# Fewer input buffers, more output buffers, stores held back: a WKV recurrence on one core

## The chip, the cores and the metric

The kernel runs on one core of a Trainium2 chip. Its time is the device time of one execution in microseconds; the median of three runs counts. All data start and end in HBM.

## What is computed

The reference is the WKV recurrence of an RWKV layer, for 16 batches, 2048 steps and 256 channels, all float32. Each batch and channel has a running numerator `aa`, a running denominator `bb` and a running maximum `pp` that keeps the exponentials in range:

```python
for t in range(seq_len):
    kk, vv = k[b, t], v[b, t]
    ww = u + kk
    qq = np.maximum(pp, ww)
    e1, e2 = np.exp(pp - qq), np.exp(ww - qq)
    output[b, t] = (e1 * aa + e2 * vv) / (e1 * bb + e2 + 1e-08)
    ww = pp - w + kk
    qq = np.maximum(ww, kk)
    e1, e2 = np.exp(ww - qq), np.exp(kk - qq)
    aa, bb, pp = e1 * aa + e2 * vv, e1 * bb + e2, qq
```

So an output is a quotient of two weighted sums over all earlier steps, with weights that are exponentials of k and of the decay w. k and v are 33.6 MB each, and so is the output: 100.7 MB have to pass between HBM and the core's memory.

## The kernel before

**Tiles.** The 2048 steps are cut into 16 chunks of 128 steps (the partitions), the 16 batches into four groups of four. Tile n is chunk n // 4 and group n % 4, so there are 64 tiles of 128 steps x 4 batches x 256 channels, 512 KB in float32. A tile of k, one of v and one of the output go through the core for each n.

**The work on a tile.** `load_k` and `load_v` bring it in (tiles `kr`, `vr`). VectorE copies k to the matmul's number format (`round_k`, L176, result `km`) and v to bfloat16 (`cast_v`, L209, result `vb`). TensorE adds the decay to k by matmuls (`logs`, L185 and L191), ScalarE takes the exponential (`exps`, L202 and L204) into the ring `EZR`, which keeps the last 12 tiles, and VectorE multiplies by v (`times_v`, L214). `sums` (L238) adds a chunk up for the state, and a chain of small steps, from `copy_sums` to `state_next`, carries the state to the next chunk and puts it into a spare row of the `EZR` tiles by four small DMAs (`inject`, L331). Ten slots after `exps` (LAG) the tile is finished: the denominator by matmuls with a triangular matrix (`den`, L341), its inverse on ScalarE as exp(-log) (`den_log` L346, `den_exp` L349, tile `rd`), the numerator by matmuls (`num`, L358), the product on VectorE (`mult`, L362, in place in `rd`) and `store` (L365).

**Loops and order.** A slot is one pass of one of two loops: n from 0 to 9, which only fills the ring, and n from 10 to 63, which also finishes tile q = n - 10 (and multiplies tile qp = n - 11). After slot 63 a tail written out by hand finishes tiles 53 to 63. Every instruction is issued in the order written (`K`), each engine works its own list from the front, and engines wait for each other by semaphores. Thus SyncE (SP), which issues all loads and all stores except two halves at the end, works one list too: at the head of slot n come `load(n + AHEAD)`, that is v(n + 5) and k(n + 6), and then `store(qp - 2)`, the store of tile n - 13. The last state injection goes through SyncE as well, the other ones through GpSimd.

**Buffers.** Tiles come from pools. A load into a buffer waits until the earlier tile in it has been read: `kpool` has AHEAD = 6 buffers, `vpool` 5. `rpool` has 8 `rd` buffers; the logarithm that opens a new `rd` waits until the earlier output in that buffer has been stored. Each of these tiles takes 4 KB of every partition, so the three pools hold 19 tiles together. k(n + 2) is copied in slot n, so a buffer of k is free two slots ahead of its number; v is cast unevenly: tiles with n % 4 of 3 and 0 in slot n, those with 1 and 2 in the slot before. Beside the buffers, each DMA of SyncE waits until the eighth one before it has landed, as eight semaphores are used in turn.

**The end.** Tile 63 is finished in two halves, so that its last bytes leave soon. For each half: exponential of that half of the denominator on ScalarE, multiply on VectorE, then two stores of 128 KB, one issued by SyncE and one by ScalarE (L533).

Of the kernel before, what the change touches and what calls it, by code (L numbers as in the profile page):

```python
# [15 lines left out]
def kernel(  # L16
# [16 lines left out]
    D = 2 * Dm  # L33
    NP = 4 * NST
    RING = 12
    AHEAD = 6
    LAG = 10
    RS = 2.0 ** -20
    CAP = 54.0
# [1 line left out]

    consts = ctx.enter_context(tc.tile_pool(name="consts", bufs=1))
    kpool = ctx.enter_context(tc.tile_pool(name="kpool", bufs=AHEAD))
    vpool = ctx.enter_context(tc.tile_pool(name="vpool", bufs=5))
    vbpool = ctx.enter_context(tc.tile_pool(name="vbpool", bufs=4))
    rpool = ctx.enter_context(tc.tile_pool(name="rpool", bufs=8))
    small = ctx.enter_context(tc.tile_pool(name="small", bufs=2))
    tiny = ctx.enter_context(tc.tile_pool(name="tiny", bufs=1))
    ps = ctx.enter_context(tc.tile_pool(name="ps", bufs=1, space=bass.MemoryType.PSUM))
# [4 lines left out]
    def rows_of(x, n):  # L54
        c, p = divmod(n, 4)
        return x[4 * p:4 * p + 4, c * TC:(c + 1) * TC, :].rearrange("n t d -> t n d")

    def load_k(n, queue=SP):
        kr_of[n] = kpool.tile([128, 4, Dm], F32, tag="kr", name="kr")
        K(queue.dma_start(out=kr_of[n], in_=rows_of(k, n)))  # L60

    def load_v(n, queue=SP):
        vr_of[n] = vpool.tile([128, 4, Dm], F32, tag="vr", name="vr")
        K(queue.dma_start(out=vr_of[n], in_=rows_of(v, n)))


    def load(n):
        if n - 1 < NP:
            load_v(n - 1)
        if n < NP:  # L70
            load_k(n)
# [37 lines left out]
    load_v(0)  # L109
    for n in range(2, AHEAD):  # L110
        load_k(n)
# [36 lines left out]
    def out_matrices(*names):  # L148
        if "L" in names:
            for h in range(2):  # L150
                fill(Lx[HS * h:HS * h + HS, HS * (1 - h):HS * (2 - h)], 0.0)
        for name in names:
            x, f = I1 if name[0] == "I" else Lx, RS if name[-1] == "N" else 1.0
            mats[name] = matrix(name, BF16)
            K(DVE.tensor_single_scalar(mats[name], x, f, op=ALU.mult))
# [18 lines left out]
    def round_k(n):  # L174
        km = consts.tile([128, 4, Dm], F32R, tag=f"km{n % 2}", name="km") if n < 2 else KM[n - 2]
        K(DVE.tensor_copy(km, kr_of.pop(n)))  # L176
        KM[n] = km

    def logs(n):
        km = KM[n].rearrange("p (i n) d -> p i (n d)", i=2)  # L180

        def rows(q):
            for i in range(2):
                g = 32 * (2 * q + i)
                K(PE.matmul(half(n, q)[:, i, :], CO[g:g + 32, :],  # L185
                            WU[g:g + 32, :].unsqueeze(1).broadcast_to([32, 2, Dm]), start=True, stop=False,
                            tile_position=(g, 0), skip_group_check=True))

        def steps(q):
            for i in range(2):  # L190
                K(PE.matmul(half(n, q)[:, i, :], (NLE, NLZ)[q], km[:, i, :], start=False, stop=True,  # L191
                            skip_group_check=True))

        rows(0)
        rows(1)
        steps(0)
        steps(1)

    def exps(n):
        if n < TURNS:  # L200
            for q in range(2):
                K(SC.activation(ez(n)[:, q], half(n, q), ACT.Exp))  # L202
        else:
            K(SC.activation(ez(n)[:, 0:2], PS[:, 0:4, :].rearrange("p (q i) x -> p q i x", q=2), ACT.Exp))  # L204

    def cast_v(n):
        vb = vbpool.tile([128, 4, Dm], BF16, tag="vb", name="vb")
        vr = vr_of.pop(n)
        K(DVE.tensor_copy(vb, vr))  # L209
        VB[n] = vb  # L210

    def times_v(n):
        vb = VB.pop(n).rearrange("p (i n) d -> p i (n d)", i=2)
        K(DVE.tensor_mul(ez(n)[:, 2:4], ez(n)[:, 0:2], vb.unsqueeze(1).broadcast_to([128, 2, 2, D])))  # L214
# [16 lines left out]
    def sums(n):  # L231
        c, p = divmod(n, 4)
        t = MISC[:, 0:Dm]
        for o in range(2):
            x = 24 - 16 * o - 2 * p
            for j in range(4):
                q, i = divmod(j, 2)
                K(PE.matmul(t[32 * j:32 * j + 32, :], mats["OH"][:, x:x + 32],  # L238
                            ez(n)[:, 2 * q, i, Dm * o:Dm * o + Dm],
                            start=p == 0 and o == 0, stop=p == 3 and o == 1,  # L240
                            tile_position=(0, 32 * j), skip_group_check=True))

    def copy_sums(c):
        ts = tiny.tile([128, Dm], F32, tag="ts", name="ts")
        if c == NST - 1:
            K(DVE.tensor_copy(ts, MISC[:, 0:Dm]))
        else:
            K(SC.activation(ts, MISC[:, 0:Dm], ACT.Copy))
        st[c, "ts"] = ts
# [88 lines left out]
    def den(n, bank=DENB):  # L338
        for m, q in (("L", 0), ("Id", 1)):
            for i in range(2):  # L340
                K(PE.matmul(bank[:, i, :], mats[m], ez(n)[:, q, i, :], start=q == 0, stop=q == 1,  # L341
                            skip_group_check=True))
# [5 lines left out]
    def den_exp(n, i=slice(0, 2)):  # L348
        K(SC.activation(RD[n][:, i, :], RD[n][:, i, :], ACT.Exp, scale=-1.0))  # L349

    def recip(n, between):
        den_log(n)
        between()
        den_exp(n)

    def num(n, bank, i):
        for m, q in (("LN", 2), ("IdN", 3)):
            K(PE.matmul(bank, mats[m], ez(n)[:, q, i, :], start=q == 2, stop=q == 3, skip_group_check=True))  # L358

    def mult(n, bank, i):  # L360
        rd = RD[n]
        K(DVE.tensor_mul(rd[:, i, :], bank, rd[:, i, :]))  # L362

    def store(n):
        K(SP.dma_start(out=rows_of(out, n), in_=RD.pop(n).rearrange("p i (n d) -> p (i n) d", n=2)))  # L365
# [22 lines left out]
    def small_work(n, where):  # L388
        for f, c in later.pop((n, where), []):
            f(c)  # L390
# [13 lines left out]
    for n in range(LAG):  # L404

        load(n + AHEAD)
        exps(n)
# [14 lines left out]
        if n < 4:  # L422
            (state_start, lambda: out_matrices("L"), lambda: out_matrices("IdN", "LN"),
             lambda: out_matrices("Id"))[n]()

    def inverses(n):
        q, qp = n - LAG, n - LAG - 1
        if qp >= 0:
            num(qp, NUMB, 1)

        sums(n - 1)
        if n + 1 < NP:
            recip(q, lambda: small_work(n, "recip"))

    for n in range(LAG, NP):

        q, qp = n - LAG, n - LAG - 1
        load(n + AHEAD)

        if qp >= 2:  # L440
            store(qp - 2)
        if qp >= 0:
            num(qp, NUMB, 0)
        den(q)
        small_work(n, "nums")
        exps(n)
        small_work(n, "act")
        if qp >= 0:
            mult(qp, NUMB, 0)
        small_work(n, "mid")  # L450
        if n == LAG:

            inverses(n)
            small_work(n, "early")
        if n + 2 < NP:
            round_k(n + 2)

        if n % 4 in (3, 0):
            cast_v(n)
        if n + 1 == NP:  # L460
            times_v(n)
        elif n % 4 < 2:
            cast_v(n + 1)
        if n > LAG:
            inverses(n)
        if qp >= 0:
            mult(qp, NUMB, 1)
        small_work(n, "scan")
        if n + 1 < NP:
            times_v(n)  # L470
            small_work(n, "chain")
            logs(n + 1)
        small_work(n, "pe")
# [4 lines left out]
    q, c = NP - LAG - 1, NST - 1  # L478
# [10 lines left out]
    den(q + 1, dbank(q + 1))  # L489
    sums(NP - 1)  # L490
    copy_sums(c)
    store(q - 2)
    store(q - 1)
    den_exp(q)
    den_log(q + 1, dbank(q + 1))
    tile_num(q, 0)
# [30 lines left out]
    n, p = NP - 1, (NP - 1) % 4  # L527
    for i in range(2):
        den_exp(n, slice(i, i + 1))
        mult(n, nbank(n, i), i)  # L530
        for j, eng in ((0, SP), (1, SC)):
            b = 4 * p + 2 * i + j
            K(eng.dma_start(out=out[b, c * TC:(c + 1) * TC, :], in_=RD[n][:, i, Dm * j:Dm * j + Dm]))  # L533
# [31 lines left out]
```

## Time and profile before

| | |
|---|---|
| time, median of 3 runs (lowest, highest) | 289.56 us (289.51, 289.62) |
| span of the profiled run | 288.0 us |
| busy: VectorE, TensorE, ScalarE | 262.3, 261.4, 254.7 us (91, 91, 88%) |
| HBM read, written | 67.12 MB, 33.55 MB |
| mean rate over the span | 350 GB/s |
| DMA issues of 512 KB | 64 of k, 64 of v, 63 of the output |
| median from issue to landing: k, v, output | 8.3, 8.3, 8.1 us |
| last k: issued, copied | 242.1, 250.4 us |
| last multiply starts | 283.5 us |

The time is that of an unprofiled run, the span goes from the first to the last instruction of the profiled one, so the two differ by some 1.5 us. Three engines and the DMA engines are all busy for most of the span; which of them holds up the others changes along the way, so the profile has to be read by stretches. A DMA has three times in the trace: the issue (an instruction on SyncE, ScalarE or GpSimd), the packets on the 16 DMA engines, and the landing, when its semaphore is complete. In a timeline the two numbers ahead of an instruction are its start and its busy time in us, SPq and ACTq are the DMA issues of SyncE and ScalarE, and a bracket behind it gives the idle time of the engine just before and the instruction that ended it.

### The profile page before, as it was taken

Reading aid. Unit: us, or ns where it says so; the run is one execution under the profiler, and the core shown is the slowest. Engines: PE = TensorE matmul, PEld = TensorE weight load, DVE = VectorE, ACT = ScalarE, POOL = GpSimd, SP = SyncE. Lnnn points to the kernel's source line nnn. Section 1 sums busy time; section 2 is a strip of 40 time slices with the busy share of each in tenths; the row PEclk is TensorE's granted clock in tenths of the full one; section 3 lists DMA queues with packets and bytes.
Section 4 is the critical chain, followed back from the end, with each engine's and each line's share of the span. In section 5 each row is a group of like instructions: output and inputs, shape, how many; then the busy total and the mean of one; then the engine's idle time right before and its main releaser. Section 6 shows DMA issues by size and latency. Waiting matters only on the chain. (4 is left out here: it accounts for less than half of the span.)

```text
span 288.0 us, 5023 instructions
## 1 busy us (share of the span) xinstructions
PE 261.4 (91%) x1694; PEld 119.4 (41%) x1694; DVE 262.3 (91%) x463; ACT 254.7 (88%) x252; POOL 105.2 (37%) x208
## 2 busy tenths in 40 slices
PE   5997897999999999999999999899998989998990
PEld 1443443544444544435444444344344444433430
DVE  4698999999999999999999999998999999988863
ACT  2675678999999999999999989999998999998891
POOL 7000523352534454543525364460434435233000
PEclk9799999999999999999999999999999999999997
DMA  6999999999999999999999999999999999994697
GB/s 214 353 348 350 349 331 349 331 361 375 381 369 381 372 379 378 381 379 381 378 376 381 369 381 375 377 376 371 373 374 380 374 377 380 373 383 160 201 339 245
DMA packets 103587, 101.54 MB, mean 353 GB/s; under 512 B 4285, under 2 KB 103561, under 8 KB 103561
## 3 DMA queue, kind: packets, MB, share of 16 engines
q1 hardware_dynamic: 101336, 100.45, 102.6%
q0 software_dynamic: 1920, 0.50, 0.8%
q8 instruction: 13, 0.21, 0.3%
q10 hardware_dynamic: 304, 0.27, 0.3%
q14 instruction: 14, 0.11, 0.1%
HBM read 67.12 MB, written 33.55 MB: 350 GB/s over the span
## 5 line engine op out<-in xcount | busy, mean ns | idle before, releaser
L204 ACT ACTIVATE EZR<-PS 128x2048 bf16<-128x2048 f32 x54 | 101.2, 1875 | 7.5 <-PE PS L191 6.5
L362 DVE TENSOR_TENSOR rd<-PS,rd 128x512 f32<-128x512 f32 x128 | 87.0, 687 | 6.1 <-ACT rd L349 4.7
L214 DVE TENSOR_TENSOR EZR<-EZR,vb 128x2048 bf16<-128x2048 bf16 x64 | 78.1, 1220 | 2.2 <-ACT EZR L202 1.5
L349 ACT ACTIVATE rd<-rd 128x1024 f32<-128x1024 f32 (+1 forms) x65 | 67.9, 1047 | 2.7 <-DVE rd L362 1.8
L346 ACT ACTIVATE rd<-PS 128x1024 f32<-128x1024 f32 x64 | 65.7, 1026 | 0.8 <-PE PS L341 0.8
L358 PE MATMUL PS<-EZR,LN 128*128 128x512 bf16 x128 | 48.7, 381 | 12.2 <-DVE rd L362 8.4
L331 POOL DMA_DIRECT2D EZR<-cb x60 | 36.5, 614 | 52.1 <-DVE cb L326 45.4
L176 DVE CAST km<-kr 128x1024 fp32r<-128x1024 f32 x64 | 44.7, 699 | 6.9 <-DMA kr<-in_k_dram 6.4
L191 PE MATMUL PS<-km,NLE 128*128 128x512 f32 x128 | 47.5, 453 | 2.3 <-DVE km L176 2.2
L358 PE MATMUL PS<-EZR,IdN 128*128 128x512 bf16 x128 | 48.4, 378 | 0.0
L209 DVE CAST vb<-vr 128x1024 bf16<-128x1024 f32 x64 | 43.4, 694 | 0.7 <-DMA vr<-in_v_dram 0.7
L191 PE MATMUL PS<-km,NLZ 128*128 128x512 f32 x128 | 40.6, 398 | 0.0
L341 PE MATMUL PS<-EZR,Id 128*128 128x512 bf16 x128 | 38.1, 379 | 0.0
L341 PE MATMUL PS<-EZR,L 128*128 128x512 bf16 x128 | 38.1, 379 | 0.0
L185 PE MATMUL PS<-WU,CO 32*128 32x512 bf16 x256 | 27.2, 388 | 3.4 <-DVE WU L400 2.2
L269 POOL TENSOR_TENSOR F<-LL,LL 128x32 f32<-128x32 f32 x13 | 6.7, 515 | 61.9 <-ACT LL L260 61.9
L191 PEld LDWEIGHTS PS<-km,NLZ 128*128 128x128 f32 x128 | 24.4, 191 | 5.8
L191 PEld LDWEIGHTS PS<-km,NLE 128*128 128x128 f32 x128 | 19.3, 190 | 17.3 <-issue 12.9
L238 PE MATMUL PS<-EZR,OH 128*32 128x256 bf16 x512 | 26.1, 278 | 0.1
L202 ACT ACTIVATE EZR<-PS 128x1024 bf16<-128x1024 f32 x20 | 19.4, 1019 | 7.6 <-PE PS L191 7.6
L358 PEld LDWEIGHTS <-IdN 128*128 128x128 bf16 x128 | 12.5, 97 | 28.7 <-issue 26.3
L282 POOL TENSOR_TENSOR Q<-P,F 128x64 f32<-128x64 f32 x13 | 15.7, 1205 | 15.0 <-DVE P L273 15.0
(71 smaller groups left out, 200.0 us busy)
## 6 DMA issues: line engine op xcount, KB each, us to landing
kr<-in_k_dram SPq DMA_DIRECT2D x64, 512.0 KB, 8.3
vr<-in_v_dram SPq DMA_DIRECT2D x64, 512.0 KB, 8.3
out_dram<-rd SPq DMA_DIRECT2D x63, 512.0 KB, 8.1
EZR<-cb POOLq DMA_DIRECT2D x60, 8.0 KB, 5.3
out_dram<-rd SPq DMA_DIRECT2D x2, 128.0 KB, 2.7
out_dram<-rd ACTq DMA_DIRECT2D x2, 128.0 KB, 2.2
EZR<-cb SPq DMA_DIRECT2D x4, 8.0 KB, 1.9
wuf<-in_w_dram ACTq DMA_DIRECT2D x1, 8.0 KB
```

The costliest lines, as they stand in the source:

```text
L176: K(DVE.tensor_copy(km, kr_of.pop(n)))
L185: K(PE.matmul(half(n, q)[:, i, :], CO[g:g + 32, :], WU[g:g + 32, :].unsqueeze(1).broadcast_to([32, 2, Dm]), start=True, stop=False, tile_p ...
L191: K(PE.matmul(half(n, q)[:, i, :], (NLE, NLZ)[q], km[:, i, :], start=False, stop=True, skip_group_check=True))
L204: K(SC.activation(ez(n)[:, 0:2], PS[:, 0:4, :].rearrange("p (q i) x -> p q i x", q=2), ACT.Exp))
L209: K(DVE.tensor_copy(vb, vr))
L214: K(DVE.tensor_mul(ez(n)[:, 2:4], ez(n)[:, 0:2], vb.unsqueeze(1).broadcast_to([128, 2, 2, D])))
L331: K(queue.dma_start(out=EZR[r:r + 1, 2 * q, r0:r0 + 4, :, :].rearrange("o p i (b x) -> o (p i b) x", b=4), in_=cb[x:x + 32, :]))
L341: K(PE.matmul(bank[:, i, :], mats[m], ez(n)[:, q, i, :], start=q == 0, stop=q == 1, skip_group_check=True))
L346: K(SC.activation(RD[n], bank, ACT.Ln, scale=RS))
L349: K(SC.activation(RD[n][:, i, :], RD[n][:, i, :], ACT.Exp, scale=-1.0))
L358: K(PE.matmul(bank, mats[m], ez(n)[:, q, i, :], start=q == 2, stop=q == 3, skip_group_check=True))
L362: K(DVE.tensor_mul(rd[:, i, :], bank, rd[:, i, :]))
```

## The change

The three pools keep their 19 tiles, divided otherwise: four for k, four for v, eleven for outputs. Loads go out four slots ahead (three for v). Stores are held back: at the head of slot n the tile n - 18 is stored instead of n - 13. Once no loads are left (from slot 61) three stores a slot are issued, of tiles whose product is ready, until they have caught up, and the tail stores what is left. The purpose is to give the loads the place in SyncE's queue that early stores took, and to leave stores for the end, when nothing is loaded. Besides, at the very end both exponentials of tile 63 are issued ahead of its first multiply and its stores.

```diff
-    AHEAD = 6
+    AHEAD = 4
+    OUTS = 11
+    LATE = 7
...
-    vpool = ctx.enter_context(tc.tile_pool(name="vpool", bufs=5))
+    vpool = ctx.enter_context(tc.tile_pool(name="vpool", bufs=AHEAD))
     vbpool = ctx.enter_context(tc.tile_pool(name="vbpool", bufs=4))
-    rpool = ctx.enter_context(tc.tile_pool(name="rpool", bufs=8))
+    rpool = ctx.enter_context(tc.tile_pool(name="rpool", bufs=OUTS))
...
+    stored = 0
+
...
         q, qp = n - LAG, n - LAG - 1
         load(n + AHEAD)
-
-        if qp >= 2:
-            store(qp - 2)
+        while stored < min(qp, max(qp - LATE + 1, stored + 3 if n + AHEAD > NP else 0)):
+            store(stored)
+            stored += 1
...
     copy_sums(c)
-    store(q - 2)
-    store(q - 1)
+    for n in range(stored, q):
+        store(n)
     den_exp(q)
...
     for i in range(2):
         den_exp(n, slice(i, i + 1))
+    for i in range(2):
         mult(n, nbank(n, i), i)
         for j, eng in ((0, SP), (1, SC)):
```

## The prediction

> **What bounds the kernel now.** I read the page's slices of DMA first.
>
> ```profile
> DMA  6999999999999999999999999999999999994697
> GB/s 214 353 348 350 349 331 349 331 361 375 381 369 381 372 379 378 381 379 381 378 376 381 369 381 375 377 376 371 373 374 380 374 377 380 373 383 160 201 339 245
> ...
> q1 hardware_dynamic: 101336, 100.45, 102.6%
> ```
>
> The DMA engines are full from the second slice (7.2 us each) to the 36th; only slices 37 and 38 (259 to 274 us) have a hole. One queue, SyncE's, carries 100.45 MB of it. So who is second? Busy time by stretch (time, then busy us and count for PE, weight load, DVE, ACT, POOL, then clock, DMA share, GB/s):
>
> ```profile
> 20.00:57.00 37.00, 32.23 (x228) 15.42 (x227) 34.87 (x64) 28.82 (x33) 11.29 (x20) 1.00 1.10 342
> 60.00:148.00 88.00, 86.02 (x578) 39.89 (x577) 87.20 (x145) 86.95 (x83) 38.03 (x71) 1.00 1.09 377
> 152.00:250.00 98.00, 91.09 (x602) 41.65 (x601) 92.25 (x151) 92.08 (x88) 40.81 (x75) 1.00 1.09 376
> ...
> 264.00:266.00 2.00, 1.29 (x6) 0.39 (x4) 1.89 (x9) 2.00 (x4) 0.00 (x0) 1.00 0.11 32
> 268.00:270.00 2.00, 2.00 (x11) 0.94 (x10) 1.60 (x3) 2.00 (x3) 0.00 (x0) 1.00 0.09 14
> 271.00:286.00 15.00, 9.70 (x43) 4.00 (x41) 9.02 (x14) 10.58 (x13) 0.00 (x0) 0.94 1.02 337
> ```
>
> From 60 to 148 us VectorE and ScalarE are 99% busy; from 152 to 250 us both are 94% busy at the same bytes per second. So compute sets the pace first and data sets it later. The same two stretches for the first consumer of k, the copy into km (VectorE's count is the last one in brackets):
>
> ```profile
> 79.10:142.70 63.60, 19.14 (x65) 10.77 (x65) 10.94 (x16) 1.00 1.09 378
> 152.20:250.40 98.20, 27.51 (x92) 15.48 (x92) 16.47 (x24) 1.00 1.09 376
> ```
>
> 16 copies in 63.6 us are 3.975 us a slot: the compute pace. From the first of the 24 to the last are 98.1 us for 23 slots, 4.265 us: the data's pace. A slot moves three tiles of 512 KB (k, v, out), so a tile takes 4.265/3 = 1.42 us. The second stretch loses 23 x (4.265 - 3.975) = 6.7 us to data. That it is k is seen from its copies between 150 and 252 us:
>
> ```profile
>   DMA kr<-in_k_dram: 4.9, 14
> ...
> DMA to landing us min/median/max: 8.0/8.3/8.6
> ```
>
> Each k lands as its copy starts: the last was issued at 242.1 us, landed 8.3 us later at 250.3, and was copied at 250.37. Last, the end, on SyncE's queue and then on ScalarE and VectorE:
>
> ```profile
> 244.84 1.28 SPq L64 DMA_DIRECT2D vr<-in_v_dram  x1
> 246.21 19.11 SPq L365 DMA_DIRECT2D out_dram<-rd  x9
> 266.77 2.52 SPq L331 DMA_DIRECT2D EZR<-cb  x4
> 269.39 12.80 SPq L365 DMA_DIRECT2D out_dram<-rd  x9
> ```
>
> ```profile
> 282.38 0.36 ACTq L533 DMA_DIRECT2D out_dram<-rd  x1
> 282.80 0.63 ACT L349 ACTIVATE rd<-rd 128x512 f32<-128x512 f32 x1 [1.84 <-DVE rd L362]
> 283.46 0.69 DVE L362 TENSOR_TENSOR rd<-PS,rd 128x512 f32<-128x512 f32 x1 [1.11 <-ACT rd L349]
> ```
>
> The last v is issued at 244.8 and lands at 253.1; from then on only stores are left, and between about 259 and 271 us the DMA engines wait for outputs. DMA time is lost there, while loads were late before it.
>
> **What the Trainium skill says.** "DMA: Bandwidth & Descriptors", "Queues, rings and completion order": SyncE owns one row of rings over the 16 engines and each engine takes descriptors in ring order. The trace agrees: a k and the v behind it both land 8.3 us after their issue. So a load's arrival follows from its place in SyncE's program, if the queue is never empty. Same page, "Anatomy of one DMA": about 2.0 us fixed for each DMA beside its bytes (there for GpSimd's path). Here an 8 KB injection from SyncE took 1.9 us on an idle queue and a 512 KB store 3.0 us (issued at 264.9), so a tile that meets an empty queue starts some 3.0 - 1.5 = 1.5 us after its issue. "Perfetto Trace Analysis", "DMA Instruction — HWDGE": an issue's window runs from satisfied semaphores to written descriptors and contains no data movement, except that a full buffer holds it up. That explains 1.28 us issues under load and 0.37 us ones at 276 to 282 us. Bandwidth I take from the trace.
>
> **The change part by part.** I write k63 for the last k tile; slot n is one pass of the main loop.
>
> *Places in the queue.* Before, slot n issues v(n+5), k(n+6), then store n-13; k63 has the stores up to 43 ahead of it, 44 of them. Afterwards slot n issues v(n+3), k(n+4), then store n-18, and k63 (slot 59) has the stores up to 40 ahead: 41. Five slots of delay, less two of shorter prefetch, are three stores fewer: 3 x 1.42 = 4.27 us sooner, for k63 and for v63 alike.
>
> *A longer read-only start.* The first store moves behind six more loads (place 47 of SyncE's program, not 41). Reads alone go at 342 GB/s, 1.53 us a tile, against 1.42 in the mix: 6 x 0.11 = 0.7 us lost.
>
> *Four buffers: a new wait.* v(n+3) now needs the cast of v(n-1), and k(n+4) and a store are queued behind it on SyncE. k's own buffer is no wait: k(n) is copied in slot n-2. Casts are uneven over four slots: v13, v14, v15, v16, v17, v18, v19 start at 50.2, 53.8, 62.0, 65.5, 66.1, 69.7, 77.9 us. So SyncE stops after k19, issued behind v18, until v15's cast ends at 62.7. The queue then holds reads until 63.9 (the landing of k19 before), and v19 can start at 62.7 + 1.5 = 64.2: 0.3 to 0.5 us of empty engines. The same sum gives 0.5 us ahead of v20 (cast v16 ends 66.2) and 0.6 us ahead of v23 (cast v19 ends 78.6, queue dry by about 79.5). Walking through all slots with 1.53, 1.42 and 1.5 us I get 1.6 us, and none later: once stores take part, three tiles need 4.27 us and compute gives 3.975, so the queue deepens by itself. Bounds: 0.8 us if reads go at 1.56, 2.6 us at 1.50. I take 1.6. No engine stalls in these gaps, as k19's copy is at 69.1; the price is DMA time, which comes due at k63.
>
> Sum for k63: 4.27 - 0.7 - 1.6 = 2.0 us sooner, at 248.3. Compute can follow: at 3.975 from 148.5 us it would be at k63's copy at 243.9, so 6.5 us is the ceiling and data still decide.
>
> *Eleven output buffers.* The logarithm of tile m (L346) needs store m-11 landed. That store stands one tile behind k(m+11). For m = 52: k63 at 250.3 + 1.4 = 251.7, the logarithm starts at 254.5: hidden by 2.8 us. In the tail, tile 63 needs store 52, about 266, against 278.4. Nothing.
>
> *Catching up, three a slot from slot 61.* 22 stores (42 to 63) follow v63, not 19. Tiles 42 to 53 are 12 x 1.37 us (385 GB/s, the store-only rate at 253 to 259 us) = 16.4 us from v63 at 251.1: done at 267.5. They fill the hole instead of ending later. The injection (L331) is behind them: issued at 264.8 to 266.7, so its last part lands at about 268.6, unloaded or behind store 53. Before it landed at 270.6 and the denominator of tile 60 ran at 271.4, now 269.4. 0.8 us spare, nothing charged; at 1.55 us a store (337 GB/s, the rate at the end) it would be overrun by 0.4 us.
>
> *Last exponentials together.* ScalarE's second half exponential no longer waits for the first half's multiply and ACT issue: it can start 1.8 us sooner (the bracket above), and the last multiply, third in a row on VectorE, starts at 282.4 instead of 283.46: 1.1 us. But the DMA share from 271 to 286 us is full at 337 GB/s; the last 256 KB cannot leave before the tiles ahead. Between 0 and 1.1 us; I take 0.1.
>
> Total: 289.56 - 2.0 - 0.1 = **287.5 us**.
>
> **The rivals.** (a) *The queue never runs dry and reads cost no more*: 4.3 us, 285.3. For it: the loads of 44 to 58 us had 9 us of queue ahead of them. With compute as the only limit the ceiling of 6.5 us gives 283.1, but that needs more stores moved than three. (b) *Too few buffers*: a queue of one or two tiles is also slower per tile, and gaps recur every fourth slot, eating all 4.3 us: 289.5, no change. For it: 337 GB/s with short queues at the end against 385 with long ones. Against it: those gaps need compute as the slower side, which ends when stores start. (c) *Slower: the injection gets stuck.* If stores are still queued as deep as 8.3 us, it lands 6.4 us later than unloaded; less the 0.8 us and some 0.4 us by which ScalarE is behind, PE waits 5.2 us: 287.5 + 5.2 = 292.7. Against it: no loads are left to refill the queue, and stores come no faster than outputs.
>
> **How the numbers follow.** Forecast 0.55, (a) 0.20 with the ceiling, (b) 0.15, (c) or another new wait 0.10. The bounds of the gaps (0.8 to 2.6) and of the exponentials (0 to 1.1) give 286.0 to 288.5 around the forecast; reaching into (a) and (b) makes 285.6 to 289.3. Faster by over 0.58 us: 0.55 + 0.20 + a quarter of (b), 0.79; same 0.11; slower 0.10.
>
> **What would show it.** Right: k63's copy near 248.3; k copies in the last third still waiting on DMA; DMA slices below 9 near 60 to 80 us; slices 37 and 38 fuller; ScalarE's 1.84 us wait gone with little from it. Wrong: k copies at 3.975 us to the end (a); SyncE waiting on casts after 80 us (b); PE waiting on the injection near 270 us (c).

## The result, and the profile after

The changed kernel takes 292.95 us (median of 4 runs, 291.94 to 293.72); the kernel before takes 289.59 us beside it (289.51 to 290.03). The ratio is 1.0111 with a 95% interval of 1.0075 to 1.0146: slower by about 3.2 us, where 2.1 us less were forecast. The profiled runs are 290.9 and 288.0 us long.

The page's slices of the DMA engines after the change:

```profile
DMA  7999999979999999999999999999999999999597
GB/s 217 355 348 350 349 332 348 338 224 336 357 309 381 362 380 377 379 375 380 376 372 382 371 380 378 377 373 367 370 376 377 368 367 373 367 384 349 183 338 240
```

Slice 37 is full, as the change meant it (349 GB/s against 160), and in exchange there is a hole in slice 9 (58 to 65 us, 224 GB/s) and shallower ones behind it. The copies of k, in the same two stretches as before (the engines are PE, weight load and VectorE; the copies are counted in the last bracket):

```profile
79.30:142.90 63.60, 19.13 (x66) 10.77 (x65) 10.94 (x16) 1.00 1.08 368
152.20:252.50 100.30, 27.52 (x92) 15.47 (x92) 16.26 (x24) 1.00 1.08 373
```

The compute pace is unchanged: 16 copies in 63.6 us. The last k is copied at 252.4 us; before it was 250.4, and 248.3 was forecast. From there to the last landing the kernel before takes 36.0 us (to 286.4), the changed one 36.7 us (to 289.1). So of the 2.9 us by which the span grew, 2.0 were lost ahead of the last k, 0.7 after it, and 0.2 lie behind the last landing.

**Ahead of the last k.** These are windows of 4 us; the last column is the rate in GB/s, the one before it the DMA share. First the kernel before:

```profile
60.00:64.00 4.00, 3.88 (x29) 1.72 (x28) 3.96 (x8) 3.87 (x4) 2.21 (x4) 1.00 1.09 364
64.00:68.00 4.00, 3.88 (x29) 2.10 (x28) 4.00 (x7) 4.00 (x5) 0.92 (x3) 1.00 1.09 370
80.00:84.00 4.00, 3.89 (x28) 2.09 (x27) 4.00 (x7) 4.00 (x5) 0.82 (x3) 1.00 1.09 366
```

Then the changed kernel, with the first of the holes in windows of half a microsecond:

```profile
60.00:64.00 4.00, 3.74 (x28) 1.73 (x28) 3.93 (x10) 3.87 (x5) 1.98 (x3) 1.00 0.63 199
64.00:68.00 4.00, 3.89 (x29) 2.10 (x28) 4.00 (x7) 4.00 (x5) 1.15 (x4) 1.00 0.88 266
80.00:84.00 4.00, 3.88 (x28) 2.08 (x27) 4.00 (x7) 4.00 (x5) 1.03 (x3) 1.00 0.94 259
...
61.00:61.50 0.50, 0.39 (x5) 0.27 (x5) 0.50 (x2) 0.50 (x1) 0.00 (x0) 1.00 1.10 350
61.50:62.00 0.50, 0.38 (x1) 0.10 (x1) 0.50 (x2) 0.50 (x2) 0.00 (x0) 1.00 0.65 205
62.50:63.00 0.50, 0.50 (x5) 0.30 (x2) 0.50 (x2) 0.47 (x2) 0.50 (x1) 1.00 0.42 123
63.50:64.00 0.50, 0.50 (x4) 0.16 (x3) 0.50 (x2) 0.40 (x2) 0.50 (x2) 1.00 0.11 15
64.50:65.00 0.50, 0.50 (x4) 0.20 (x2) 0.50 (x2) 0.50 (x1) 0.41 (x2) 1.00 0.34 78
65.50:66.00 0.50, 0.50 (x10) 0.12 (x8) 0.50 (x2) 0.50 (x2) 0.00 (x0) 1.00 1.07 376
```

VectorE and ScalarE are as busy as before throughout: neither stalls while the queue is dry. The price is bytes. Added up from the start, the changed kernel's packets (in tiles of 512 KB) are level with those of before at 56 us, 1.1 tiles behind at 64 us, 2.2 at 72, 2.7 at 80 and 3.5 at 84 us. Then it stays nearly level: 3.8 at 150 us, 4.3 at 252 us.

What emptied the queue is in SyncE's timeline (SPq are DMA issues; L66 loads v, L62 loads k) and in its list of waits (time in all, times, longest):

```profile
55.28 1.41 SPq L62 DMA_DIRECT2D kr<-in_k_dram  x1
62.95 0.37 SPq L66 DMA_DIRECT2D vr<-in_v_dram  x1
63.37 1.09 SPq L62 DMA_DIRECT2D kr<-in_k_dram  x1
```

```profile
SPq L66 <- DVE vb L211: 25.5, 13, 6.2
```

SyncE stands 6.2 us in one wait, from the end of k19's issue at 56.7 us to the end of the cast of v15 at 62.9 us; before the longest wait on a cast was 1.1 us. An emptied queue comes back slowly: the k issued behind v19, at 63.37 us, lands 5.9 us later (the first line has the issue, the last its landing):

```profile
L62 SPq DMA_DIRECT2D kr<-in_k_dram x1: 1088/1088/1088, 63.4 to 63.4; - x1
...
DMA to landing us min/median/max: 5.9/5.9/5.9
```

**After the last k.** The chain in order of time (start, duration, what) goes through the state injection for tiles 56 to 59, issued by GpSimd:

```profile
260.39 0.28 DVE cb L328
260.67 0.29 issue
260.95 0.43 POOL EZR L333
261.39 0.15 issue
261.53 5.37 DMA EZR<-cb
266.90 0.14 issue
267.04 1.04 PE PS L343 x4
```

Issue to landing of its four small DMAs after the change, and then before:

```profile
DMA to landing us min/median/max: 5.4/5.5/5.6
```

```profile
DMA to landing us min/median/max: 3.0/3.5/4.0
```

The held-back stores keep the DMA engines full to 269 us, and these 8 KB pieces land beside them about 2 us later. TensorE waits 1.5 us for them (`PE PS L343 <- DMA EZR<-cb: 1.5, 1, 1.5` in the list of waits), and the logarithm of tile 57 comes 0.7 us later, counted from k63. The end itself:

```profile
282.07 2.13 ACT L351 ACTIVATE rd<-rd 128x1024 f32<-128x1024 f32 x3
283.20 2.48 DVE L364 TENSOR_TENSOR rd<-PS,rd 128x512 f32<-128x512 f32 x4 [0.57 <-ACT rd L351]
285.11 1.41 SPq L538 DMA_DIRECT2D out_dram<-rd  x2
```

The exponentials now follow one another, and the last multiply ends 33.3 us after the start of k63's copy rather than 33.8; but the last landing comes 3.4 us after that multiply rather than 2.3.

### The profile page after: what moved, and what is told of

It is laid out like the page before. It is cut to its first block, busy times and chain, and to the rows that moved or that the text cites. A ratio compares the mean times of both kernels' runs of the same rounds, so it can differ in the third digit from the quotient of the medians.

```text
span 290.9 us, 4989 instructions
## 1 busy us (share of the span) xinstructions
PE 256.3 (88%) x1662; PEld 119.1 (41%) x1694; DVE 262.3 (90%) x463; ACT 255.0 (88%) x252; POOL 105.5 (36%) x208
## 5 line engine op out<-in xcount | busy, mean ns | idle before, releaser
L178 DVE CAST km<-kr 128x1024 fp32r<-128x1024 f32 x64 | 44.5, 695 | 8.9 <-DMA kr<-in_k_dram 8.2
L360 PE MATMUL PS<-EZR,IdN 128*128 128x512 bf16 x112 | 42.4, 378 | 0.0
L343 PE MATMUL PS<-EZR,L 128*128 128x512 bf16 x128 | 38.1, 379 | 1.5 <-DMA EZR<-cb 1.5
L343 PE MATMUL PS<-EZR,Id 128*128 128x512 bf16 x115 | 35.3, 379 | 0.0
```

## The experiments

My theory after the result: holding the stores back and cutting v to four buffers is good for three places in the queue, as forecast, but together they leave the queue empty once, at 60 to 70 us, and again at 80 us, for much longer than I worked out; late stores also delay an injection a little. Rivals: late stores cost time of themselves; the fewer k buffers do it; the new end does it; the delayed injection is the greater part. Ratios are to the kernel before on the same chip, with the 95% interval; times are medians. Three groups ran on three chips, so that absolute times of different groups are not compared. A profile shows a single execution, and that need not be a middling one: it was the fastest of all runs of its kernel for the end alone, for four stores put into the hole and for one store before the long wait, and the slowest for the fifth k buffer and for LATE = 8.

**The end alone**, on the kernel before.

```diff
     for i in range(2):
         den_exp(n, slice(i, i + 1))
+    for i in range(2):
         mult(n, nbank(n, i), i)
```

> The kernel before with one part of the change alone: both exponentials of tile 63 ahead of its multiplies and stores. Theory A (the loss of the changed kernel comes from an empty DMA queue between 61 and 84 us and from the injection near 265 us, not from this edit; the DMA engines are full to the end): 289.6 us within 0.3, with the last multiply some 1.1 us earlier and the last landing unmoved. Rival B (the end is set by the engines): 288.5 us, last landing 1.1 us earlier. Rival C (the edit itself costs): over 290.2 us.

Measured: 289.95 us (22 runs), 1.0015 [1.0005, 1.0024]. The last multiply ends 1.6 us earlier in the profile (282.5 against 284.1 us) and the last landing only 0.5 us. The gain is given back ahead of the last landing, where the DMA engines are full, and by the medians the edit has no part in the loss beyond 0.4 us.

**Late stores alone**, on the kernel before with its six, five and eight buffers.

```diff
-        if qp >= 2:
-            store(qp - 2)
+        if qp >= 4:
+            store(qp - 4)
...
-    store(q - 2)
-    store(q - 1)
+    for n in range(q - 4, q):
+        store(n)
```

> The kernel before with its six, five and eight buffers, and stores held back by two slots more (tile n - 15 in slot n), all else as before. Theory A: late stores gain and it is the buffers that lost; the last k has 42 stores ahead of it, not 44, so it lands 2 x 1.42 us less some 0.3 us for slower reads sooner, near 247.9 us; no dry stretch before 246 us; the injection for tiles 56 to 59 a little later; 287.3 us (286.8 to 288.2). Rival D (late stores lose by themselves, as they crowd the end): 289.6 us or more.

Measured: 292.92 us (6 runs), 1.0115 [1.0092, 1.0139]. My forecast missed. The last k landed at 249.6 us but was copied only at 254.2: data were early, and compute was late. The reason is in the list of waits, where ScalarE's logarithm waits for a store:

```profile
ACT rd L346 <- DMA out_dram<-rd: 5.5, 20, 0.5
```

Each wait is at most 0.5 us, but there are 20, and from 110 us on the copies of k come only every 4.2 us on average instead of 3.975. Eight output buffers don't bear a store two slots later. A store stands in the queue behind the loads issued ahead of its slot, and its landing frees the buffer for the logarithm OUTS tiles later. With loads A slots ahead and stores D slots late, the traces fit an A + D that stays below OUTS + 12: before 6 + 13 = 19 against 20 and after the change 22 against 23, both without such waits, here 21 against 20. So this run put a wait of its own in place of the one to be tested. What it does show is why late stores had to be paid with input buffers. Nor is its queue full throughout:

```profile
64.00:68.00 4.00, 3.89 (x33) 1.72 (x32) 4.00 (x7) 3.91 (x4) 3.13 (x6) 1.00 0.85 248
68.00:72.00 4.00, 3.96 (x28) 2.08 (x21) 4.00 (x7) 4.00 (x6) 0.00 (x0) 1.00 0.82 257
```

By 72 us it is 2.0 tiles behind the kernel before, with five v buffers; SyncE stands 5.1 us in one wait for a cast of v. This execution is one of those in which TensorE's clock dipped at 48 to 51 us (see the end), so the hole can't be put down to the late stores alone.

**A fifth v buffer**, on the changed kernel (one `vb` buffer, half as large, is given up for it).

```diff
-    vpool = ctx.enter_context(tc.tile_pool(name="vpool", bufs=AHEAD))
-    vbpool = ctx.enter_context(tc.tile_pool(name="vbpool", bufs=4))
+    vpool = ctx.enter_context(tc.tile_pool(name="vpool", bufs=5))
+    vbpool = ctx.enter_context(tc.tile_pool(name="vbpool", bufs=3))
```

> The changed kernel with a fifth buffer for v, paid for by a third instead of a fourth buffer of the bfloat16 copy of v, which only VectorE writes and reads; v(n + 3) then waits for the cast of tile n - 2 and not n - 1. Theory A: the dry stretch at 61 to 84 us goes; the last k still has 41 stores ahead of it and lands near 247 us, not 252.4; about 287.5 us (286.5 to 289). Rival D (late stores or short queues lose by themselves): over 291 us, k landing after 251.

Measured: 288.1 us (22 runs), 0.9955 [0.9938, 0.9971]: faster than before. The last k is copied at 247.8 us, 4.6 us earlier than in the changed kernel. The three windows of above and the one from 68 us on, in this kernel:

```profile
60.00:64.00 4.00, 3.88 (x29) 1.68 (x27) 3.93 (x9) 3.92 (x4) 2.13 (x4) 1.00 1.09 348
64.00:68.00 4.00, 3.89 (x28) 2.09 (x27) 4.00 (x7) 4.00 (x5) 0.99 (x3) 1.00 1.10 341
68.00:72.00 4.00, 3.96 (x27) 1.74 (x26) 4.00 (x7) 3.97 (x5) 1.54 (x3) 1.00 1.05 325
80.00:84.00 4.00, 3.89 (x29) 2.09 (x27) 4.00 (x7) 4.00 (x5) 0.87 (x3) 1.00 1.07 367
```

The holes are gone in this execution, and what is left is reads at 341 to 348 GB/s against 364 to 370 in the mix of before, and 325 against 379 from 68 to 72 us. By 72 us this kernel is 0.74 tile behind that of before. SyncE's longest wait for a cast of v is 3.2 us. TensorE still waits 1.3 us for an injection (5.2 to 5.5 us to landing), though the loss is gone, so that is not the greater part of it.

**A fifth k buffer instead**, as the control.

```diff
-    kpool = ctx.enter_context(tc.tile_pool(name="kpool", bufs=AHEAD))
+    kpool = ctx.enter_context(tc.tile_pool(name="kpool", bufs=5))
...
-    vbpool = ctx.enter_context(tc.tile_pool(name="vbpool", bufs=4))
+    vbpool = ctx.enter_context(tc.tile_pool(name="vbpool", bufs=3))
```

> The control for the fifth v buffer: the same space (from the third instead of fourth bfloat16 copy) given to k, five buffers for k and four for v, all else as in the changed kernel. Theory A (the queue is emptied by v's wait for a cast, with k and stores behind it): nothing is won, the dry stretch at 61 to 84 us stays, 293 us (292 to 294). Rival E (any buffer more helps, or the smaller bfloat16 pool does): about 288 us, as with the fifth v buffer.

Measured: 293.37 us (4 runs), 1.0121 [1.0093, 1.0149]. No gain, and the hole stays:

```profile
60.00:64.00 4.00, 3.89 (x29) 1.78 (x28) 3.85 (x10) 4.00 (x6) 0.98 (x3) 1.00 0.95 302
64.00:68.00 4.00, 3.88 (x26) 1.60 (x24) 4.00 (x6) 3.90 (x5) 3.13 (x6) 1.00 0.44 94
```

SyncE's longest wait for a cast of v is 7.3 us here. (Part of the depth of this hole belongs to a dip of TensorE's clock at 46 to 50 us, which the profiled run of the changed kernel doesn't have; the times don't depend on this one run.) So it is v's buffer, not k's and not the one taken from `vb`, that stops SyncE.

**Four stores put into the hole**, on the changed kernel with its four v buffers: the same stores, only earlier.

```diff
+        while stored < {16: 2, 18: 3, 20: 4}.get(n, 0):
+            store(stored)
+            stored += 1
         load(n + AHEAD)
```

> The changed kernel with its four buffers, but four stores put into the dry stretch: two ahead of the load of v19 (slot 16), one ahead of v21, one ahead of v23; the later stores and the 41 ahead of the last k are as in the changed kernel. Theory A: these four use time in which the queue was empty, some 3 of the 4.3 us that the last k lost come back, it lands near 249 us, time 290 us (289 to 291). Rival D: no better than the changed kernel, 292 us or more.

Measured: 291.27 us (8 runs), 1.0066 [1.004, 1.0093]; the last k at 250.0 us. That is above the 289 to 291 us that I had forecast. By the ratios some 40% of the loss comes back with the buffers unchanged, though the two intervals overlap; the profile shows it more plainly: the windows 64 to 68 and 80 to 84 us now have 336 and 311 GB/s, and 1.2 tiles are lost by 84 us instead of 3.5. The rest didn't come back because a hole opens later: SyncE waits 3.1 us for a cast of v again, from 94 to 100 us the rate is 263 to 311 GB/s, and the profile is 2.5 tiles behind by 104 us.

**Four k and four v buffers alone**, on the kernel before, with its stores where they were.

```diff
-    AHEAD = 6
+    AHEAD = 4
...
-    vpool = ctx.enter_context(tc.tile_pool(name="vpool", bufs=5))
+    vpool = ctx.enter_context(tc.tile_pool(name="vpool", bufs=AHEAD))
```

> The kernel before with four buffers each for k and v and nothing else changed (eight output buffers, stores as before, old end): the other half of the change alone. 46 stores are ahead of the last k instead of 44. Theory A (v's wait empties the queue only where reads alone fill it; here stores begin at 56 us and fill it): no more than 0.7 of a tile is lost at 60 to 84 us, the last k lands 2 x 1.42 us less 0.4 us later, near 252.8 us, time 292 us (291.3 to 293). Rival L (four buffers empty the queue whatever the stores do): 3 tiles lost there as in the changed kernel, 294.5 us or more.

Measured: 292.96 us (6 runs, 291.99 to 296.44), 1.0106 [1.0075, 1.0136]. As slow as the changed kernel, for another reason. Its queue does not run dry:

```profile
60.00:64.00 4.00, 3.74 (x28) 1.64 (x28) 3.93 (x10) 3.97 (x4) 1.16 (x2) 1.00 1.07 376
64.00:68.00 4.00, 3.88 (x27) 1.75 (x26) 4.00 (x7) 3.90 (x5) 1.98 (x5) 1.00 1.09 377
80.00:84.00 4.00, 3.88 (x26) 1.76 (x25) 4.00 (x7) 3.88 (x5) 1.87 (x5) 1.00 1.09 380
```

The last k now stands behind two stores more (46), 2 x 1.42 = 2.8 us; it is copied at 253.4 us against 250.4. From here to the changed kernel the stores move by five slots, 5 x 1.42 = 7.1 us of places, and k63 comes only 1.0 us earlier (252.4). The other 6.1 us are what holding the stores back costs when v has four buffers: reads alone, and an empty queue. So four buffers alone don't empty the queue: while stores run, they keep the DMA engines busy as v waits for its cast, here for at most 3.0 us at a time. Whether late stores alone would empty it is open: the run for that did, but with a clock dip.

**How late the stores should be, with five v buffers.** One kernel with LATE = 5, one with LATE = 8 (the changed kernel and the one above have 7).

```diff
-    LATE = 7
+    LATE = 5
```

> The kernel with the fifth v buffer and stores two slots less late (tile n - 16 in slot n): 43 stores ahead of the last k instead of 41. Theory A (places in the queue set the last k): the last k lands 2 x 1.42 us less 0.4 us for fewer reads at the slower rate later, near 250.2 us instead of 247.8, less up to 1 us if the rest of the dry stretch is filled; time 290 us (289.3 to 290.6). Two stores fewer are in the queue when the injection for tiles 56 to 59 is issued, which lands some 4 us after its issue instead of 5.4. Rival D (late stores do not matter or lose): 288 us or less.

```diff
-    LATE = 7
+    LATE = 8
```

> The kernel with the fifth v buffer and stores one slot later (tile n - 19 in slot n): 40 stores ahead of the last k. Theory A: 1.42 us sooner, less 0.25 us for slower reads and up to 1 us of new dry time: the last k near 246.8 us, time 287 to 288. Rival F (the eleven output buffers bind: the store of tile m lands when k(m + 21) does, in the slot before the logarithm of tile m + 11 or in its own, as with two slots later stores and eight buffers): ScalarE waits on stores at L348 and it is slower than 288.1 us, up to 292.

Measured: LATE = 5 gives 289.65 us (20 runs), 0.9999 [0.9979, 1.0019], k63 at 250.4; LATE = 8 gives 288.56 us (20 runs), 0.9962 [0.9947, 0.9976]. So two stores fewer ahead of k63 are worth about 0.4% (1.2 us where two places are 2.8), and the third adds nothing. With 23 against 23 in the sum above, ScalarE begins to wait for output buffers, as the rival had it:

```profile
ACT rd L348 <- DMA out_dram<-rd: 2.8, 11, 0.3
```

Whether that is what used up the third place isn't shown: the profiled run, the slowest of the 20, also has a clock dip and is 3.6 tiles behind by 88 us.

**The old end with five v buffers.**

```diff
     for i in range(2):
         den_exp(n, slice(i, i + 1))
-    for i in range(2):
         mult(n, nbank(n, i), i)
```

> The kernel with the fifth v buffer and the old end (exponential, multiply and stores of one half, then of the other). In the kernel before the edit of the end alone cost 0.4 us. Theory G (the edit costs, as the last bytes gather at the end of a full queue): 287.7 us. Rival H (the edit is within noise of nothing): 288.1 us within 0.3. Rival B (it gains where the queue is deeper): 288.5 us or more.

Measured: 288.47 us (15 runs), 0.9961 [0.9941, 0.9981]. Not to be told from 0.9955: the end is worth nothing here either.

**One store before the long wait, with five v buffers.**

```diff
+        if n == 17:
+            store(0)
+            stored = 1
         load(n + AHEAD)
```

> The kernel with the fifth v buffer, and its first store one slot earlier (slot 17, ahead of the load of v20), put where its queue still ran dry for 0.8 of a tile at 64 to 72 us; 41 stores ahead of the last k as before. Theory A: the last k lands up to 1.0 us sooner than at 247.8, time 287.3 us (286.8 to 288). Rival I (the rest of the dry stretch costs nothing): 288.1 us as without it.

Measured: 288.52 us (16 runs; before 289.84 beside it), 0.994 [0.9915, 0.9965]; k63 at 246.6 us, span 284.7 us. It has the best ratio of all, but the intervals of the five-buffer kernel with and without this store overlap. So it isn't decided whether the store gains; the 246.6 us belong to the fastest of the 16 runs.

**The delayed injection from ScalarE's queue**, with five v buffers.

```diff
-                (s + 4, "nums", turn_back), (s + 4, "mid", inject), (s + 4, "mid", state_next)]
+                (s + 4, "nums", turn_back), (s + 4, "mid", (lambda c: inject(c, SC)) if c == NST - 2 else inject),
+                (s + 4, "mid", state_next)]
```

> The kernel with the fifth v buffer and the injection for tiles 56 to 59 issued by ScalarE, on a queue of its own, instead of GpSimd. Theory J (GpSimd's injection lands late, 5.4 us after its issue, as it shares the DMA engines with held-back stores, and TensorE waits for it): if a queue without a backlog of its own is served in turn, it lands 2 to 3.5 us after its issue and TensorE's wait for it at L343 goes; ScalarE loses four issues of about 0.4 us and up to 0.5 us of waiting for the copy, so the time is within 1 us of 288.1. Rival K (any queue is as slow beside a full one): it lands 5 us after its issue and TensorE still waits.

Measured: 291.87 us (7 runs), 1.0072 [1.0039, 1.0106]. Another queue doesn't help beside full DMA engines: the four small DMAs land 4.9 us after their issue, as the rival said, and now ScalarE itself has to issue them and then waits for them:

```profile
L333 ACTq DMA_DIRECT2D EZR<-cb x4: 510/514/629, 258.8 to 262.9; - x4
...
ACT rd L348 <- DMA EZR<-cb: 4.8, 1, 4.8
...
DMA to landing us min/median/max: 4.9/4.9/5.0
```

In the kernel with four buffers alone, which has no stores held back, the same injection lands after 1.7 to 1.8 us on idle DMA engines. So it is the load on these engines, not the queue, that sets its time. The 291.87 us are not the price of this edit alone: the profiled run copies k63 at 250.5 us, 2.7 us later than the kernel with five v buffers, though up to there both run the same program.

**Five k, five v and ten output buffers**, with stores five slots late.

```diff
-    AHEAD = 4
-    OUTS = 11
-    LATE = 7
+    AHEAD = 5
+    OUTS = 10
+    LATE = 5
```

> Five buffers for k, five for v, ten for outputs (the space of the third instead of fourth bfloat16 copy), stores in slot n of tile n - 16: 42 stores ahead of the last k, loads five and four slots ahead. Theory A: no dry queue at all, the last k near 247.9 us, 288.1 us; and as loads wait less on VectorE's progress, executions spread less than the 287 to 291 us seen with four k and five v buffers. Rival M (fewer stores ahead are all that counts): one store more than there, 288.1 + 1.2 = 289.3 us with the same spread.

Measured: 289.74 us (14 runs), 0.9993 [0.9967, 1.002]. No gain over the kernel before: nearer to the 289.3 us of the rival, for which the stores ahead of k63 are all that counts, than to the 288.1 of my theory. The profile is 1.0 tile behind by 72 us, where I had expected no dry queue. Its times spread as widely (287.69 to 291.58) as those of the other kernels with five v buffers. I had expected more prefetch to narrow the spread; it didn't.

## Why the prediction was wrong

**The step that failed** is "Four buffers: a new wait": "it can start at 62.7 + 1.5 = 64.2: 0.3 to 0.5 us of empty engines", and so 1.6 us for all gaps. The wait itself came where the step put it: v19 was held by v15's cast, to 62.9 us where 62.7 was forecast, then v23 by v19's at 78.8 us. Only the size of the gaps was wrong, for two reasons:

- The end of the old data. I took the landing of k19 (63.9 us) as the moment until which the queue holds reads. The rate in the half-microsecond windows falls from 350 to 205 GB/s at 61.5 us already, and is 15 GB/s just before k19 lands, at 64.0 us here. So most of the bytes had moved well ahead of the landing.
- The start of the new data. I took 1.5 us from issue to flow, which I had from a 512 KB *store* that landed in 3.0 us. The first *read* of the kernel, on an idle queue, took 4.1 us to land, 2.6 us more than the 1.5 us of its bytes, and that figure stood in the trace of before:

```profile
L60 SPq DMA_DIRECT2D kr<-in_k_dram x1: 447/447/447, 0.8 to 0.8; - x1
...
DMA to landing us min/median/max: 4.1/4.1/4.1
```

After the wait, v19 is issued at 62.95 us and the rate is back at 376 GB/s only at 65.5 us: 2.5 us, not 1.5. I had named the Trainium skill, "DMA: Bandwidth & Descriptors", section "Anatomy of one DMA", with its 2.0 us of setup and completion for each DMA on GpSimd's path, and set it aside for the 1.5 us; the 2.6 us of the first read, on SyncE's path, are above both.

In tiles: 3.5 are lost by 84 us. The kernel with five v buffers, which has the long read-only start but no holes, loses 0.74. (Neither profile has the later clock dip.) The difference of some 2.8, at 1.42 us a tile, is 4.0 us for the empty queue, against 1.6 us in the sum and 2.6 us as its upper bound. So even the bound was too low, as it varied the rate of the reads and kept the 1.5 us. With these two terms as measured the sum for k63 is 4.27 - 1.05 - 4.0: 0.8 us later. The 0.8 tile lost after 84 us, 1.1 us, makes up the rest of the 2.0.

**The other steps.** *Places in the queue*: right. Four tiles and a quarter behind and three places ahead make 1.25 x 1.42 = 1.8 us later, where the trace has 2.0; and with five v buffers the three places brought k63 2.6 us ahead of that of before. *A longer read-only start*: 0.7 us forecast, 0.74 tile or 1.05 us at most. *Eleven output buffers*: nothing, as forecast, though only by one slot in the sum shown above. *Last exponentials together*: nothing, nearly as forecast (0.1 us); 0.4 us slower alone.

*Catching up*: I charged nothing, since the last injection (tiles 60 to 63, through SyncE's queue) had 0.8 us to spare. That one was no stall. But the one before it (tiles 56 to 59, through GpSimd) I did not look at, and it cost most of the 0.7 us after the last k. This part of it rests on the trace: the run that was to take it away put a longer wait in its place.

**The rivals.** The time measured, 292.95 us, is nearly the 292.7 us of rival (c), "the injection gets stuck", which had at most 0.10, but that is a coincidence. Its mechanism gives at most 0.7 us of the loss instead of 5.2 us, and at another injection than the one it named. The mechanism was that of (b), "too few buffers", and its limit of 4.3 us was the wrong one: gaps can cost more than the places bring, and then the change is slower than before. The case against (b), that gaps end when stores start, held from 84 us on. By then the bytes were lost, and as the last third waits for data (`DVE km L178 <- DMA kr<-in_k_dram: 8.2, 20, 1.3`), they were not caught up. Still open is why another 0.8 tile is lost between 84 and 252 us, half of it after 230 us.

## What to carry to other kernels

Where one queue carries loads and stores, moving stores back only pays if the loads can fill the queue alone meanwhile: count the buffers of each load against the longest wait for its consumer, not against the mean. A gap in the queue costs from where the bytes end, ahead of the last landing, to where the rate is back, and both are read from windows of half a microsecond; take the start-up from a read on an idle queue in the same trace. Here the fifth v buffer, at the price of one (half as large) of the bf16 copy, turned 1.1% slower into 0.45% faster than before (288.1 us), with every other part of the change left as it was. Its times spread wider than those of before, though, and a profile of one execution can show a better queue than the median has.

## What the runs showed of the hardware that was not expected

- A read into an emptied queue is slow to come back: 2.5 us from issue to the full rate, and 5.9 us from the issue of the second tile to its landing. Ahead of that the rate ran down over 2.5 us (61.5 to 64.0 us), with the mean busy share of the DMA engines at 0.65, then 0.42, then 0.11. The first read of the kernel lands 4.1 us after its issue, a store on idle engines after 3.0 us.
- In the injection for tiles 56 to 59 an 8 KB DMA lands 1.7 us after its issue on idle engines and 4.9 to 5.6 us after it beside full ones, from GpSimd's queue as from ScalarE's.
- TensorE's granted clock dips to half for some 3 us between 46 and 52 us in some profiled runs and not in others. These are the lines of the kernels with one store before the wait and with LATE = 5:

```profile
PEclk9999999999999999999999999999999999999996
```

```profile
PEclk9799997999999999999999999999999999999997
```

With LATE = 5 the granted clock is 0.50 from 46 to 48 us and 0.70 from 48 to 50 us, right after a stretch of 2 us in which TensorE is busy for 0.2 us. The kernel with LATE = 7 and five v buffers is about as idle in that stretch (0.4 us) and keeps 1.00, so this idle time alone doesn't decide it. With the dip a slot there takes 1.4 us longer (4.96 us from one cast of v to the next, against 3.54). The kernel before ran 288.7 to 290.6 us in nearly all of its runs, the one with one store before the wait 286.4 to 290.7 us. That a shallow queue passes such a delay on to the loads, where a deep one hides it, fits the profiles: with the dip three kernels with five v buffers lose 1.9 to 2.2 tiles by 72 us, against 0.74 without, and of the pair that runs the same program up to 250 us the one with the dip copies k63 2.7 us later. But other kernels with the dip lose only 0.4 and 1.0 tile, and it was not tried by itself.
